# A 90 degree rotation of an 8192 x 8192 matrix: half of the outputs of most macro tiles turned by VectorE and ScalarE, and small transfers two outputs later

## The chip, the cores and the metric

The kernel runs on one core of a Trainium2 chip. The core has five engines that take instructions in order from queues of their own: PE (TensorE), DVE (VectorE), ACT (ScalarE), POOL (GpSimd) and SP (SyncE, which here only issues DMAs and waits). Semaphores order them. Sixteen DMA engines move data between the device memory and the on-chip memory SBUF (128 partitions). The metric is the device time of one execution in microseconds (us), lower is better.

## The reference

The input is a float32 matrix of 8192 x 8192 (256 MiB) and k, which is always 1:

```python
def reference(x, k):
    return np.rot90(x, k)
```

So `out[8191 - c, r] = x[r, c]`: the matrix is transposed and its row order is reversed. Nothing is computed; each element is read once and written once, 268 MB each way.

## The kernel before

The matrix is cut into 16 macro tiles of 1024 rows by 4096 columns (`kk` counts them). A macro tile is loaded by T = 8 loads of 128 rows (2 MB, 16 KB in each partition; `m` counts all 128 loads) and leaves as J = 8 outputs (`n` counts them), each one block of 512 output rows by 1024 output columns, 2 MB. Output j of a macro tile needs the chunk j (512 columns) of each of its eight loads.

The path of the data:

- SP issues the loads (L178). Two landing buffers take turns (LAND); three others hold outputs (OUTS). SP issues the next load into a buffer once VectorE has copied the previous one out of it (semaphore `s_rev`).
- VectorE copies each load, with the columns of each chunk in reverse order, into a ring of 63 slots of 512 columns (L248). A macro tile has 64 chunks, one more than there are slots. A slot is free when TensorE has transposed what it held: load m = n + 8 fills the slots that output n held. The first seven chunks wait for all of output n (`s_half`), the last one waits until the next output has begun (`s_first`), since the ring is one slot short.
- TensorE transposes 128 x 128 blocks out of the ring into PSUM (L279): 32 for each output, 16 in each of two halves (`ps0`, `ps1`). It waits for the eviction of the same half of the output before (`s_ev`).
- ScalarE evicts each half, 128 x 2048, from PSUM into an output buffer (L317), waits ahead of it until the buffer's last store has landed, and issues the store (L326).

SP's queue carries the loads and ScalarE's queue the stores, so that both directions share the sixteen DMA engines.

The last macro tile is cut otherwise, so that the end is short: its outputs take four loads (512 output columns) and two chunks each, and five buffers take turns. One of its outputs is split in two. The first part (`n_few`, the third of the last nine, n = 122) has only 64 partitions and is written by sixteen small transfers of 32 KB that SP issues (L220) behind the last load; the rest, 1.5 MB, is an output of its own (n = 123). The output that comes five later takes the same buffer and waits for all sixteen (`s_few`).

The lines in question:

```python
            begin = wide if kk == KK - 1 else 1
            cuts = [0, begin, J - 1, J] if t == T - 1 else [0, J - 1, J]
...
                got.append((lo, hi, first if hi == J else full if lo == 0 else None))
```

Of the kernel before, what the change touches and what calls it, by code (L numbers as in the profile page):

```python
# [6 lines left out]
P = 128  # L7
# [3 lines left out]
T = R // P  # L11
W = 4096
G = 4
J = W // (G * P)
# [3 lines left out]
CH = G * P  # L18
F = G * R
SLOTS = T * J - 1  # L20

END = T // 2

H = 2
# [28 lines left out]
def slot(kk, t, j):  # L53

    at = t * J + j if kk % 2 == 0 else J + t + j * T
    return (at + kk // 2 * (J + 1)) % SLOTS


def kernel(tc: tile.TileContext, x: bass.AP, k: bass.AP, out: bass.AP):
# [19 lines left out]
    n_few = n_out - J + 2  # L79
    kk, ts, js = outs[n_few]  # L80
    assert len(js) == 2 and END * P * H * G == F
    blocks = [(j, g * P, P) for j in reversed(js) for g in range(G)]
    few = [[(js[-1], g * P // 2 + h * FEW, P // 2) for g in range(G)] for h in range(H)]
    outs[n_few] = (kk, ts, js, few)
    outs.insert(n_few + 1, (kk, ts, js, [blocks[2 : 2 + G], blocks[2 + G :]]))
    n_out += 1

    def halves(n):
        if len(outs[n]) == 4:
            return outs[n][3]  # L90
        blocks = [(j, g * P, P) for j in reversed(outs[n][2]) for g in range(G)]
        return [blocks[: len(blocks) // H], blocks[len(blocks) // H :]]


    order = [(kk, a, b) for kk in range(KK) for a in range(T) for b in range(J)]
    for i, (kk, t, j) in enumerate(order):
        if i >= SLOTS:
            pk, pj, pt = order[i - SLOTS]
            assert slot(kk, t, j) == slot(pk, pt, pj)

    with tc.tile_critical():  # L101
# [9 lines left out]
        ]  # L111

# [4 lines left out]
        s_first = nc.alloc_semaphore("s_first")  # L117
        s_half = nc.alloc_semaphore("s_half")
        s_ev = nc.alloc_semaphore("s_ev")
        s_few = nc.alloc_semaphore("s_few")  # L120

# [13 lines left out]

        pieces, rev = {}, {}
        done = 0
        for m in range(n_load):  # L140
            kk, t = divmod(m, T)
            got = []
            if m >= T:
                full = (s_half, H * (m - T + 1))
                first = (s_first, m - T + 2)
            else:
                full = None
                first = (s_first, 1) if t == T - 1 else None
            begin = wide if kk == KK - 1 else 1
            cuts = [0, begin, J - 1, J] if t == T - 1 else [0, J - 1, J]  # L150
            if m < T - 1:
                cuts = [0, J]
            for lo, hi in zip(cuts[:-1], cuts[1:]):
                got.append((lo, hi, first if hi == J else full if lo == 0 else None))
                done += 1
                for j in range(lo, hi):
                    rev[m, j] = done
            pieces[m] = got

        def runs(kk, t, lo, hi):  # L160

            at = [slot(kk, t, j) for j in range(lo, hi)]
            i = 0
            while i < len(at):
                n = 1
                step = at[i + 1] - at[i] if i + 1 < len(at) else 1
                if step > 0:
                    while i + n < len(at) and at[i + n] - at[i + n - 1] == step:
                        n += 1
                else:  # L170
                    step = 1
                yield lo + i, n, at[i], step
                i += n
# [14 lines left out]
        with nc.Block() as block:  # L188
# [15 lines left out]
            @block.sync  # L204
            def _(e):
                for m in range(LAND + OUTS, n_load):
                    last = [i for i in range(m) if load_buf(i) == load_buf(m)]
                    e.wait_ge(s_rev, rev[last[-1], J - 1])
                    load(e, m)
                kk, ts, js, _ = outs[n_few]  # L210
                b = out_buf(n_few)
                top = M - macros[kk][1] - (js[-1] + 1) * CH
                left = macros[kk][0] + ts[0] * P
                rows = len(ts) * P
                for h in range(H):
                    e.wait_ge(s_ev, H * n_few + h + 1)
                    for at in (0, 2 * FEW):
                        for d in range(LEFT):
                            first = top + h * FEW + at + d
                            e.dma_start(  # L220
                                out=bass.AP(
                                    tensor=out.tensor,
                                    offset=out[first : first + 1, left : left + 1].offset,
                                    ap=[[LEFT * M, FEW // LEFT], [4 * FEW * M, G], [1, rows]],
                                ),
                                in_=bufs[b][
                                    at + d : at + FEW : LEFT, h * F // H : (h + 1) * F // H
                                ].rearrange("m (g f) -> m g f", f=rows),
                            ).then_inc(s_few, 16)
                e.wait_ge(s_few, 16 * 2 * H * LEFT)  # L230
                for b in range(LAND + OUTS):
                    n = sum(out_buf(i) == b and i != n_few for i in range(n_out))
                    if n:
                        e.wait_ge(s_store[b], 16 * n)

            @block.vector
            def _(e):
                for m in range(n_load):
                    kk, t = divmod(m, T)
                    b = load_buf(m)  # L240
                    a = bufs[b][:].rearrange("p (j c) -> p j c", c=CH)
                    e.wait_ge(s_land[b], 16 * (uses_before(m, load_buf) + 1))
                    for lo, hi, wait in pieces[m]:
                        if wait:
                            e.wait_ge(*wait)
                        for j, n, at, step in runs(kk, t, lo, hi):
                            v = ring[:, at * CH : (at + (n - 1) * step + 1) * CH]
                            i = e.tensor_copy(  # L248
                                out=bass.AP(
                                    tensor=v.tensor,  # L250
                                    offset=v.offset,
                                    ap=[v.ap[0], [step * CH, n], [1, CH]],
                                ),
                                in_=a[:, j : j + n, ::-1],
                            )
                        i.then_inc(s_rev, 1)

            @block.tensor
            def _(e):
# [8 lines left out]
                for n, (kk, ts, js, *_) in enumerate(outs):  # L268
                    parts = halves(n)
                    rows = len(ts) * P  # L270

                    def transpose(t, h, b):
                        j, off, width = parts[h][b]
                        if n:
                            wait(s_ev, H * (n - 1) + h + 1)
                        wait(s_rev, rev[kk * T + t, j])
                        at = slot(kk, t, j) * CH + off
                        f = b * rows + (t - ts[0]) * P
                        i = e.transpose(  # L279
                            ps[h][:width, f : f + P], ring[:, at : at + width], ident  # L280
                        )
                        if t == ts[-1] and b == len(parts[h]) - 1:
                            i.then_inc(s_half, 1)
                        elif t == ts[0] and h == H - 1 and b == len(parts[h]) - 1:
                            i.then_inc(s_first, 1)

                    order = [
                        (t, h, b) for h in range(H) for b in range(len(parts[h])) for t in ts
                    ]
                    if js[0] == 0:  # L290
                        order.sort()
                    for t, h, b in order:
                        transpose(t, h, b)

            @block.scalar
            def _(e):
                e.wait_ge(s_id, 2)
                e.copy(scratch, ident[:, :1])  # L298
                for n, (kk, ts, js, *_) in enumerate(outs):
                    r0, c0 = macros[kk]  # L300
                    parts = halves(n)
                    rows = len(ts) * P
                    b = out_buf(n)
                    for h in range(H):
                        if h == 0:
                            stores = [i for i in range(n) if out_buf(i) == b]
                            loads = [i for i in range(n_load) if load_buf(i) == b]
                            if stores and stores[-1] == n_few:
                                e.wait_ge(s_few, 16 * 2 * H * LEFT)
                            elif stores:  # L310
                                e.wait_ge(s_store[b], 16 * sum(i != n_few for i in stores))
                            elif loads:
                                e.wait_ge(s_rev, rev[loads[-1], J - 1])
                        e.wait_ge(s_half, H * n + h + 1)  # L314
                        width = parts[h][0][2]
                        f = len(parts[h]) * rows
                        e.copy(  # L317
                            bufs[b][:width, h * F // H : h * F // H + f], ps[h][:width, :f]
                        ).then_inc(s_ev, 1)
                    if n == n_few:  # L320
                        continue
                    groups = sum(len(part) for part in parts)
                    top = M - c0 - js[0] * CH - groups * P
                    left = r0 + ts[0] * P
                    e.wait_ge(s_ev, H * (n + 1))
# [41 lines left out]
```

## Time and profile before

The median of three runs is 1264.59 us (1264.31 to 1264.68). The profile is of one execution of its own.

| | us | of the span |
|---|---|---|
| the profiled execution's own time | 1264.36 | |
| its span, first to last instruction | 1262.3 | |
| PE busy (4,120 transposes, mean 357 ns) | 726.8 | 58% |
| ACT busy (258 evictions, mean 1867 ns) | 469.7 | 37% |
| DVE busy (313 copies, mean 1337 ns) | 403.0 | 32% |
| bytes read and written | 537 MB | 425 GB/s over the span |

The page gives the share of DMA time and the rate in 40 slices of the span; a row of a group gives the line, engine, operation, shapes and count, then busy us and mean ns, and after the second bar the idle time ahead of it with what ended it. Busy time is not the bound by itself: an engine that waits for data costs nothing as long as what it waits for never stops. The granted TensorE clock was 0.766 on the mean.

### The profile page before, as it was taken

The page shows a single profiled execution, that of the slowest core. Times are in us where ns is not written, and L with a number is a line of the kernel's source. Part 1 is how long each engine was busy: PE and PEld are TensorE (multiplying, and loading weights), DVE is VectorE, ACT ScalarE, POOL GpSimd, SP SyncE. Part 2 cuts the span into 40 slices and gives each one's busy share as a digit, 9 for nine tenths or more (in the row PEclk, how much of TensorE's full clock was granted, in tenths as well). Part 3 has the DMA queues.
Part 4 walks back from the last instruction along what each step waited for, and adds up shares of the span by engine and source line. Part 5 has one row for each costly group of instructions (what it writes and reads, how often), then busy time and mean ns, then how long its engine had stood idle before and what let it go on. Part 6 is the DMA issues. An engine that isn't in the chain of part 4 may idle for free.

```text
span 1262.3 us, 9427 instructions
## 1 busy us (share of the span) xinstructions
PE 726.8 (58%) x4120; PEld 683.2 (54%) x4120; DVE 403.0 (32%) x313; ACT 469.7 (37%) x260; POOL 0.7 (0%) x6
## 2 busy tenths in 40 slices
PE   1566566665546645566555655566555655556564
PEld 1456465665545545565554655555555654556564
DVE  3323432324323343322342233422234222442210
ACT  0343333433334333433334333343333433434364
POOL 0000000000000000000000000000000000000000
PEclk9967767676787777777777776777777777777888
DMA  9999999999999999999999999999999999999998
GB/s 399 416 430 430 428 428 429 428 430 429 428 429 428 429 429 430 427 429 432 427 428 430 430 428 428 431 429 427 430 429 428 429 429 428 430 430 428 429 412 361
DMA packets 37032, 537.48 MB, mean 426 GB/s; under 512 B 4160, under 2 KB 4160, under 8 KB 4160
## 3 DMA queue, kind: packets, MB, share of 16 engines
q10 hardware_dynamic: 18432, 267.92, 50.0%
q1 hardware_dynamic: 18560, 268.97, 49.9%
q8 instruction: 32, 0.52, 0.2%
q14 instruction: 8, 0.07, 0.0%
HBM read 268.44 MB, written 268.44 MB: 425 GB/s over the span
## 4 chain that ended last, share of the span: by engine, by line
DMA 80%; issue 8%; DVE 5%; ACT 4%; PE 1%; SPq 1%; ACTq 0%
DMA buf<-in_x_dram 70%; DMA out_dram<-buf 11%; DVE ring L248 5%; ACT buf L317 4%; PE ps L279 1%; SPq L220 1%; ACTq L326 0%; SPq L178 0%; ACTq L314 0%; SPq L362 0%; SPq L101 0%
## 5 line engine op out<-in xcount | busy, mean ns | idle before, releaser
L279 PE MATMUL ps<-head,ring 128*128 128x128 f32 x4120 | 726.8, 357 | 522.7 <-ACT buf L317 462.3
L279 PEld LDWEIGHTS ps<-head,ring 128*128 128x128 f32 x4120 | 683.2, 190 | 566.1 <-ACT buf L317 497.2
L317 ACT COPY buf<-ps 128x2048 f32<-128x2048 f32 (+1 forms) x258 | 468.3, 1867 | 781.1 <-DMA out_dram<-buf 609.3
L248 DVE COPY ring<-buf 128x512 f32<-128x512 f32 (+7 forms) x313 | 403.0, 1337 | 811.4 <-DMA buf<-in_x_dram 810.1
L298 ACT ACT_TABLE_LOAD x1 | 1.3, 1283 | 0.9 <-SPq L101 0.9
L194 POOL TENSOR_SCALAR_AFFINE_SELECT head<-head 128x128 f32<-128x128 f32 x1 | 0.3, 292 | 0.2 <-POOL head L192 0.2
L192 POOL MEMSET head<- 128x128 f32 x1 | 0.2, 205 | 0.5 <-SPq L101 0.5
L298 ACT COPY head<-head 128x1 f32<-128x1 f32 x1 | 0.2, 191 | 0.0
L348 POOL MEMSET const-bfloat16-1.0<- 128x1 bf16 x1 | 0.1, 101 | 0.0
L348 POOL MEMSET const-uint8-127<- 128x1 uint8 x1 | 0.1, 101 | 0.0
L348 POOL MEMSET const-float32-0.0<- 128x1 f32 x1 | 0.1, 100 | 0.2 <-issue 0.2
L348 POOL MEMSET const-float32-1.0<- 128x1 f32 x1 | 0.1, 98 | 0.0
## 6 DMA issues: line engine op xcount, KB each, us to landing
buf<-in_x_dram SPq DMA_DIRECT2D x128, 2048.0 KB, 16.8
out_dram<-buf ACTq DMA_DIRECT2D x127, 2048.0 KB, 25.6
out_dram<-buf ACTq DMA_DIRECT2D x1, 1536.0 KB, 9.8
out_dram<-buf SPq DMA_DIRECT2D x16, 32.0 KB
```

Of the source, the lines that this page charges most:

```text
L192: e.memset(ident, 0.0).then_inc(s_id, 1)
L194: e.affine_select(out=ident, in_=ident, compare_op=mybir.AluOpType.not_equal, fill=1.0, base=0, pattern=[[-1, P]], channel_multiplier=1,). ...
L220: e.dma_start(out=bass.AP(tensor=out.tensor, offset=out[first : first + 1, left : left + 1].offset, ap=[[LEFT * M, FEW // LEFT], [4 * FEW ...
L248: i = e.tensor_copy(out=bass.AP(tensor=v.tensor, offset=v.offset, ap=[v.ap[0], [step * CH, n], [1, CH]],), in_=a[:, j : j + n, ::-1],)
L279: i = e.transpose(ps[h][:width, f : f + P], ring[:, at : at + width], ident)
L298: e.copy(scratch, ident[:, :1])
L317: e.copy(bufs[b][:width, h * F // H : h * F // H + f], ps[h][:width, :f]).then_inc(s_ev, 1)
L348: nc = _bacc.Bacc("TRN2", target_bir_lowering=False, num_devices=1)
```

## The change

**Who turns the blocks.** In macro tiles 1 to 13 the outputs j = 1, 3, 5, 7, and in macro tile 14 j = 1, 3, 5, no longer go through TensorE and PSUM. VectorE writes their chunks into the ring by its transpose of 32 x 32 blocks in place of the copy (a second instruction for each load). When an output's buffer is free, its 16 pairs of source and destination quadrant (32 partitions each) are moved from the ring into the buffer: eight copies of 32 x 1024 by VectorE and eight by ScalarE (`moves`). VectorE does its eight ahead of the load that reuses the slots, and waits for ScalarE's eight (`s_act`) before it overwrites them. ScalarE issues the store when both are done. 55 outputs move so. Macro tiles 0 and 15 go by TensorE as before.

**The ring.** Slots now hold tile and chunk in a plain order (`slot`), and the conditions on `s_first` are gone. The chunk that has no slot, the last of a macro tile's last load, is copied in reverse into the first 512 columns of its own landing buffer; TensorE transposes it from there into the last 512 columns of `ps1` (`corner`), and ScalarE copies it into the eighth output's buffer ahead of the rest (`s_corner`, `s_freed`). The landing buffer is free again once the corner is in PSUM.

**PE's outputs.** Those of macro tiles 0 to 14 now have three parts in place of two halves (2048, 1536 and 512 columns; for j = 7 2048 less one tile of each group, and so on), since the corner holds a part of `ps1`. The third part uses `ps0` after the first has been evicted. In the last macro tile TensorE's order is by halves throughout.

**The small transfers.** `n_few` becomes the fifth of the last nine outputs (n = 124); its rest is n = 125. No later output takes its buffer.

The diff, cut to its core:

```diff
+Q = 32
+BY_DVE = 8
+BY_PE = [0, 2, 4, 6]
...
 def slot(kk, t, j):
-    at = t * J + j if kk % 2 == 0 else J + t + j * T
-    return (at + kk // 2 * (J + 1)) % SLOTS
+    return t * J + j if kk % 2 == 0 else j * J + t
...
-    n_few = n_out - J + 2
+    n_few = n_out - T + END
...
+    def by_pe(kk):
+        return list(range(J)) if kk in (0, KK - 1) else BY_PE + [J - 1] * (kk == KK - 2)
...
+        def moves(n, share):
+            kk, ts, (j,), _ = outs[n]
+            rows = len(ts) * P
+            first, step, tiles = spaced([slot(kk, t, j) for t in ts if (t, j) != (T - 1, J - 1)])
+            for a, q in share:
+                yield (
+                    at(
+                        bufs[out_buf(n)][q * Q : q * Q + Q, :],
+                        a * Q,
+                        [[rows, G], [P, tiles], [1, Q]],
+                    ),
+                    at(
+                        ring[a * Q : a * Q + Q, :],
+                        first * CH + q * Q,
+                        [[P, G], [step * CH, tiles], [1, Q]],
+                    ),
+                )
...
             @block.vector
...
+                    n = m - T
+                    if n >= 0 and moved[n]:
+                        room_for(e, n)
+                        e.wait_ge(s_rev, rev[n // J * T + T - 1 - (n % J == J - 1), n % J])
+                        for to, of in moves(n, pairs[:BY_DVE]):
+                            i = e.tensor_copy(out=to, in_=of)
+                        i.then_inc(s_dve, 1)
                     e.wait_ge(s_land[b], 16 * (uses_before(m, load_buf) + 1))
...
+                    if n >= 0:
+                        if moved[n]:
+                            e.wait_ge(s_dve, moved_until(n))
+                            e.wait_ge(s_act, moved_until(n))
+                        else:
+                            e.wait_ge(s_half, turned_until(n))
+                    for js in pieces[m]:
+                        if (m, js[0]) == (n_load - 1, J - 1):
+                            e.wait_ge(s_half, turned_until(KK * J - J))
+                        if kk < KK - 1 and (t, js[0]) == (T - 1, J - 1):
+                            e.wait_ge(s_rev, rev[m, 0])
+                            e.tensor_copy(
+                                out=at(bufs[b][:], 0, [[CH, 1], [1, CH]]), in_=landed(b, js)
+                            ).then_inc(s_rev, 1)
+                            continue
+                        turn = e.transpose if in_quadrants(kk, js[0]) else e.tensor_copy
+                        turn(out=chunk(kk, t, js), in_=landed(b, js)).then_inc(s_rev, 1)
...
             @block.scalar
...
+                    room_for(e, n)
+                    if kk < KK - 1 and js[0] == J - 1:
+                        e.wait_ge(s_corner, kk + 1)
                         e.copy(
+                            at(bufs[b][:], rows - P, [[rows, G], [1, P]]),
+                            at(corner, 0, [[P, G], [1, P]]),
+                        ).then_inc(s_freed, 1)
+                    if moved[n]:
+                        e.wait_ge(s_rev, rev[kk * T + T - 1 - (js[0] == J - 1), js[0]])
+                        for to, of in moves(n, pairs[BY_DVE:]):
+                            i = e.copy(to, of)
+                        i.then_inc(s_act, 1)
+                        e.wait_ge(s_act, moved_until(n))
+                        e.wait_ge(s_dve, moved_until(n))
```

## The prediction

> **What bounds the kernel now.** I read the page first (slices, DMA queues, groups), then the groups by form, the order of time of a middle stretch, and the windows of the last 50 us. The page says that the DMA engines are never free.
>
> ```profile
> DMA  9999999999999999999999999999999999999998
> GB/s 399 416 430 430 428 428 429 428 430 429 428 429 428 429 429 430 427 429 432 427 428 430 430 428 428 431 429 427 430 429 428 429 429 428 430 430 428 429 412 361
> q10 hardware_dynamic: 18432, 267.92, 50.0%
> q1 hardware_dynamic: 18560, 268.97, 49.9%
> q8 instruction: 32, 0.52, 0.2%
> ```
>
> 537 MB go through 16 engines at 427 to 432 GB/s from slice 3 to slice 38. At a flat 429 they would need 1252.8 us of the span's 1262.3: under 10 us belong to start and end, and no engine that computes sets the middle. The last line matters too: 32 transfers of 0.52 MB, 64 bytes for each of PE's 8,240 instructions, go over the same engines.
>
> Next, how much room each engine has in a period (one 2 MB load and one 2 MB store, 9.8 us).
>
> ```profile
> 602.36 3.64 ACT L317 COPY buf<-ps 128x2048 f32<-128x2048 f32 x2 [6.12 <-DMA out_dram<-buf]
> 603.02 4.22 DVE L248 COPY ring<-buf 128x3584 f32<-128x3584 f32 x2 [5.53 <-DMA buf<-in_x_dram]
> 612.11 3.63 ACT L317 COPY buf<-ps 128x2048 f32<-128x2048 f32 x2 [6.12 <-DMA out_dram<-buf]
> 612.79 4.22 DVE L248 COPY ring<-buf 128x3584 f32<-128x3584 f32 x2 [5.55 <-DMA buf<-in_x_dram]
> ```
>
> ScalarE and VectorE both wait for DMA more than half the period. The stretch also gives the phase: the eviction at 602.36 is the third output of its group of eight, and the load that lands at 603.02 fills the slots of the second. So the load that reuses an output's slots lands 612.79 - 602.36 = 10.4 us after that output's buffer came free.
>
> Prices, and the end:
>
> ```profile
> L248 DVE COPY ring<-buf 128x2048 f32<-128x2048 f32 x17 | 20.7, 1219 | 48.4 <-DMA buf<-in_x_dram 48.4
> L248 DVE COPY ring<-buf 128x1024 f32<-128x1024 f32 x17 | 11.7, 687 | 55.7 <-DMA buf<-in_x_dram 55.7
> L317 ACT COPY buf<-ps 128x1024 f32<-128x1024 f32 x1 | 1.0, 1018 | 0.0
> ...
> 1244.00:1249.00 5.00, 3.23 (x29) 3.19 (x30) 0.00 (x0) 4.33 (x3) 0.00 (x0) 1.00 0.93 390
> 1249.00:1254.00 5.00, 0.51 (x5) 0.27 (x3) 0.00 (x0) 2.79 (x2) 0.00 (x0) 1.00 1.00 419
> ...
> 1258.00:1259.00 1.00, 0.00 (x0) 0.00 (x0) 0.00 (x0) 0.00 (x0) 0.00 (x0) 0.50 0.71 295
> 1259.00:1260.00 1.00, 0.00 (x0) 0.00 (x0) 0.00 (x0) 0.00 (x0) 0.00 (x0) 0.50 0.16 66
> ```
>
> The last two columns of a window are DMA share and GB/s. With a full store queue the end runs at 419; in other windows it has holes, and in the last two us only some engines still work.
>
> **The change, part by part.** *VectorE in the middle.* 55 outputs move (four in each of macros 1 to 13, three in macro 14). Each adds eight 32x1024 copies. The row of that length is 0.687 us; the slow end is a copy like the 128x3584 above, 4.22 - 0.43 (the 128x512 that follows it) = 3.79 us or 1.06 ns an element, so 1.15. I take 0.687, the row of equal length: 5.5 us an output (9.2 at the slow end). The Trainium skill (VectorE: DVE Perf Modes, What auto-detection actually checks) says that a one-source fp32 copy in SBUF gets the double rate where the outermost counts are both even or equal; the trace agrees (seven chunks into a merged run: 3.79 us; the same size with seven against seven: 2.19). By it every new copy, four against four, is fast; by the slow price the sum for two loads below would be 16.0 in place of 12.3.
>
> A load's chunks become one 128x2048 copy (1.22) and one 128x2048 transpose. No row shows a transpose. Ends: 1.22 (as a fast copy) and 4.3 (twice the slow copy row, as nothing here excludes two passes); I take the slow copy row, 2048 x 1.06 = 2.2, since a block transpose is no plain copy. Two loads and one moved output, 19.6 us of DMA, cost VectorE 5.5 + 2 x 3.4 = 12.3 us. The corner copy is one more 0.43 per macro, hidden.
>
> *ScalarE.* A moved output replaces two evictions (3.64) by eight copies. The 1018 ns row reads PSUM, the new ones SBUF; bounds 0.69 (VectorE's row) and 1.87 (a whole eviction); I take 1.02, so 8.2 us. A PE output now takes three evictions: rows 1.87 and 1.02 give 0.83 ns an element plus 0.17, so 1.87 + 1.44 + 0.59 = 3.9. With 0.6 for each store issue a pair of outputs takes 13.3 of 19.6 us (20.1 at the upper bound).
>
> *Waits.* VectorE now waits ahead of a load for the store buffer, and for ScalarE's copies before it overwrites slots; the load's chunks queue behind that, and behind them SyncE's next load. The moves start when the buffer comes free and end 8.2 us later, before the load lands at 10.4: cover 2.2 us. If that is gone, the load queue runs dry only after another 9.8 - 3.4 = 6.4 us, since the next load is then still under way, and even then the store queue feeds the engines. The PE outputs' slots are free once the first eviction (1.9) and four late transposes (under 1) are done, far ahead of 10.4. The old condition on the first tiles of the next output goes. A moved store is issued some 8.8 us after its buffer came free, 4.2 before, with two stores (19.6 us) still queued: hidden. In the middle all this costs 0.
>
> *TensorE.* 4,120 transposes become 256 + 13 x 132 + 160 + 280 = 2,412. Their busy time was hidden, so 0 directly. But 3,416 fewer instructions are 0.22 MB, 13 of the 32 fetches. These took 0.2% of 16 x 1262 us, 40 us (30 to 50 by rounding): 1.25 each, 17 us for 13. Some 770 more instructions on VectorE and ScalarE, at the same 64 bytes, give 2 us back. 15/16 = 0.9 us less for each engine, if it is spread evenly; the engines that end last may lose none (0) or twice that (1.9).
>
> *The end.* The sixteen small transfers (17.4 us of issue on SyncE, a 64-partition eviction pair of 3.63 and 32 half-width transposes), and the 1.5 MB output after them, go behind two full outputs. On ScalarE's queue two whole evictions pass them: at 4.32 us an output (1209.99 to 1214.31) the store now issued at 1230.24 goes at 1226.6, 3.6 earlier; the small ones start 8 us later and land, as now, up to 6 us after the last is issued: 1243.8 + 8 = 1252, before the last store. The wait for them ahead of an eviction (chain: 7.16 us up to 1243.85, of which ScalarE idled 2.7) goes, since the ring of five buffers no longer comes back to theirs. So the last store is issued about 1247 instead of 1251.8. This fills the holes: 1224 to 1227, 1236 to 1239 and 1247 to 1249 had shares 0.85, 0.86 and 0.80, or 1.3 us in all. But it shortens the run only for engines that had the holes. By the trace's landing marks twelve engines finished the last store at 1258.7 and four at 1259.8 to 1260.2. The four show no break from 1240 on: their marks of the last four stores are 5.0 us apart. One was the slowest at every store, the other three are most likely among the four that carry the small transfers (each small transfer makes four packets, which fit between their store packets). Moving the transfers doesn't lighten these. I count 0, bounds -1.3 and +1.3 (the same holes opened for the four).
>
> *Sum:* 1264.36 (profiled; 0.23 under the median) - 0.9 + 0 = 1263.5. Own range 1261.2 to 1265.7.
>
> **The rivals.** *Faster by more than 0.2%* (under 1262.06): the fetches hit the slowest engines more than others, and the end evens out too: -1.9 - 1.3 = 1261.2. For it: the landing marks of one store drift from 1.7 us apart at the start to 11.5 near the end, so something hits some engines alone. Against: the engines with the small transfers keep their load. Another way to it would be that PE's reads had slowed the packets; windows with PE busy 5.00 and 0.60 of 5 us show 426 and 436 GB/s beside the 429 mean, which is how packets fall into windows, so I give that little. The Trainium skill (SBUF — State Buffer, SBUF: two separate sides) says that engine and DMA accesses have separate ports and cannot conflict; by it that gain is nil, as in the trace.
>
> *Slower:* VectorE becomes the bound. It decides where a pair of loads and a moved output pass 19.6 us, for example 9.2 + 2 x (1.22 + 4.3) = 20.2: 0.6 us on each of 55 pairs, +33 us, 1297. One wrong price is not enough (5.5 + 11.0 = 16.5; 9.2 + 6.8 = 16.0). For it: neither operation stands in the trace. Against: both prices must be wrong at once. A milder form is ScalarE at its 1.87 bound: 20.1 us a pair, +27 us, 1291.
>
> *Slower at the end:* the small transfers land after the last store, which decides from 1258 on. ScalarE's chain would have to slip by 6 more us; each us beyond costs one, some 1268. Against: from 1210 on ScalarE never waits longer than 3.0 us at a time.
>
> *Nothing reaches the end:* the fetches saved lie on other engines: 1264.4, inside my case.
>
> **Chances.** Forecast and no effect (within 0.2%, 1262.06 to 1267.12, about what a measurement of this kernel tells from no change): 0.50. Faster rival 0.28. VectorE or ScalarE over their budget 0.12, small transfers late 0.07, a wait that I have not seen 0.03: slower 0.22. The range goes down to 1260.5 (the faster case with 0.7 us more of the end evened out) and up to 1270 (the late transfers); the overloaded engine (0.12) and some tails stay outside.
>
> **What would show it.** Right: GB/s 427 to 432 from slice 3 to 38; q8 near 19 packets; PE x2412; VectorE and ScalarE each busy 55 to 60%, VectorE still waiting for loads; the moves under 0.7 us, transposes near 2.2, ScalarE's copies near 1.0; no eviction waiting for the small transfers; last store issued near 1247. Wrong: VectorE busy without a gap, slices under 420 in the middle, SyncE's loads issued later than 8 us after a landing, a SyncE wait that ends after the last store.

## The result, and the profile after

The changed kernel takes 1267.89 us (median of ten runs, 1267.50 to 1268.07), the kernel before 1264.54 beside it: a ratio of 1.0026, 95% interval 1.0018 to 1.0035. It is slower by 3.3 us; the forecast was 1263.5 and no difference that can be measured. The profiled execution took 1268.03 us with a span of 1266.2.

The page of the changed kernel, engines' busy times, slices and DMA queues:

```profile
PE 468.6 (37%) x2412; PEld 411.2 (32%) x2412; DVE 712.1 (56%) x719; ACT 728.9 (58%) x670; POOL 0.7 (0%) x6
...
DMA  9999999999999999999999999999999999999996
GB/s 396 415 430 430 429 429 429 430 430 428 429 430 430 430 427 430 430 430 428 429 429 429 429 429 430 429 430 430 429 430 428 429 430 429 428 430 430 429 419 291
...
q8 instruction: 19, 0.31, 0.1%
q14 instruction: 16, 0.13, 0.0%
```

The middle is untouched: 427 to 430 GB/s from slice 3 to slice 38, as before. The q8 line counts the instruction fetches of PE, packets that bring an engine its next instructions: they fell from 32 to 19, as forecast. The line below it, q14, is what the prediction did not show: fetches of 8 KB, 16 in place of 8. The same line of the kernel before:

```profile
q14 instruction: 8, 0.07, 0.0%
```

The loss stands in the last slice, 291 GB/s where it was 361. The windows of the end of the kernel before (the last three columns are TensorE's granted clock, DMA share and GB/s):

```profile
1256.00:1258.00 2.00, 0.00 (x0) 0.00 (x0) 0.00 (x0) 0.00 (x0) 0.00 (x0) 0.50 0.98 410
1258.00:1260.00 2.00, 0.00 (x0) 0.00 (x0) 0.00 (x0) 0.00 (x0) 0.00 (x0) 0.50 0.43 180
1260.00:1262.00 2.00, 0.00 (x0) 0.00 (x0) 0.00 (x0) 0.00 (x0) 0.00 (x0) 0.50 0.00 0
```

The windows of the end of the changed kernel:

```profile
1254.00:1256.00 2.00, 0.00 (x0) 0.00 (x0) 0.00 (x0) 0.00 (x0) 0.00 (x0) 0.50 0.69 287
1256.00:1258.00 2.00, 0.00 (x0) 0.00 (x0) 0.00 (x0) 0.00 (x0) 0.00 (x0) 0.50 0.33 139
1258.00:1260.00 2.00, 0.00 (x0) 0.00 (x0) 0.00 (x0) 0.00 (x0) 0.00 (x0) 0.50 0.16 66
1260.00:1262.00 2.00, 0.00 (x0) 0.00 (x0) 0.00 (x0) 0.00 (x0) 0.00 (x0) 0.50 0.12 49
1262.00:1264.00 2.00, 0.00 (x0) 0.00 (x0) 0.00 (x0) 0.00 (x0) 0.00 (x0) 0.50 0.08 33
```

Before, all engines stop within some two us. After, most stop between 1255 and 1259, and from 1260 to 1262 the share is 0.12 = 2/16: two DMA engines work alone for some five us, and one of them for one more. Each of the sixteen leaves a landing mark for each store, and those of the last store say the same (us, sorted; the marks carry no engine's name):

```
before 1259.1 x8, 1259.2 x4, 1260.2, 1260.2, 1260.5, 1260.6
after  1255.5 1255.5 1255.6 1255.7 1255.7 1256.0 1256.1 1256.1 1257.1 1257.2 1257.4 1257.7 1258.6 1258.6 1263.4 1264.6
```

Fourteen engines are done earlier than before, two are 3 to 4 us later, and the last one sets the time. In every run below the median lies 3.3 to 4.0 us above the last mark of its profile.

### The profile page after: what moved, and what is told of

Read it like the earlier page. It is cut to its first block, busy times and chain, and to the rows that moved or that the text cites. A ratio compares the mean times of both kernels' runs of the same rounds, so it can differ in the third digit from the quotient of the medians.

```text
span 1266.2 us, 6966 instructions
## 1 busy us (share of the span) xinstructions
PE 468.6 (37%) x2412; PEld 411.2 (32%) x2412; DVE 712.1 (56%) x719; ACT 728.9 (58%) x670; POOL 0.7 (0%) x6
## 4 chain that ended last, share of the span: by engine, by line
DMA 78%; DVE 11%; issue 5%; ACT 3%; PE 1%; ACTq 0%; SPq 0%
DMA buf<-in_x_dram 75%; DVE ring L334 11%; DMA out_dram<-buf 4%; ACT buf L416 3%; PE ps L377 1%; DVE buf L315 0%; ACTq L428 0%; ACT buf L397 0%; SPq L247 0%; ACTq L410 0%; SPq L464 0%; SPq L126 0%; ACTq L407 0%
## 5 line engine op out<-in xcount | busy, mean ns | idle before, releaser
L377 PE MATMUL ps<-head,ring 128*128 128x128 f32 (+1 forms) x2352 | 455.8, 371 | 776.4 <-ACT buf L416 591.9
L377 PEld LDWEIGHTS ps<-head,ring 128*128 128x128 f32 (+1 forms) x2352 | 398.4, 196 | 833.5 <-ACT buf L416 637.4
L404 ACT COPY buf<-ring 32x1024 f32<-32x1024 f32 (+1 forms) x440 | 447.1, 1016 | 196.4 <-DMA out_dram<-buf 191.6
L334 DVE COPY ring<-buf 128x2048 f32<-128x2048 f32 (+4 forms) x152 | 182.4, 1201 | 496.6 <-DMA buf<-in_x_dram 493.5
L416 ACT COPY buf<-ps 128x2048 f32<-128x2048 f32 (+4 forms) x213 | 271.7, 1345 | 241.0 <-PE ps L377 117.0
L315 DVE COPY buf<-ring 32x1024 f32<-32x1024 f32 (+1 forms) x440 | 291.8, 663 | 5.3
L334 DVE STREAM_TRANSPOSE ring<-buf 128x2048 f32<-128x2048 f32 (+1 forms) x112 | 246.8, 2204 | 0.0
L397 ACT COPY buf<-ps 128x512 f32<-128x512 f32 x15 | 8.8, 585 | 79.9 <-DMA out_dram<-buf 79.9
L365 PE MATMUL ps<-head,buf 128*128 128x128 f32 x60 | 15.9, 420 | 0.0
L365 PEld LDWEIGHTS ps<-head,buf 128*128 128x128 f32 x60 | 13.0, 229 | 0.0
```

The lines of the kernel that those rows point to most:

```text
L315: i = e.tensor_copy(out=to, in_=of)
L334: turn(out=chunk(kk, t, js), in_=landed(b, js)).then_inc(s_rev, 1)
L365: i = e.transpose(corner[:, g * P : g * P + P], bufs[load_buf(m)][:, g * P : g * P + P], ident,)
L377: i = e.transpose(ps[h][:width, to : to + P], chunk(kk, t, [j])[:, 0, off : off + width], ident,)
L397: e.copy(at(bufs[b][:], rows - P, [[rows, G], [1, P]]), at(corner, 0, [[P, G], [1, P]]),).then_inc(s_freed, 1)
L404: i = e.copy(to, of)
```

## Which engines are late, and why

The time of each fetch packet can be set beside the number of instructions that an engine had run, and beside the stores in which one DMA engine fell back against the other fifteen. After, q14 has a packet at 147.8, 312.2, 473.0, 636.1, 793.2, 960.0 and 1115.9 us, where VectorE had run 61, 194, 318, 446, 570, 705 and 833 instructions, so one for each 128 or so (8 KB are 128 times 64 bytes). These counts take in the instructions that only wait. Followed from store to store by the marks, one and the same DMA engine fell back by 0.95 to 1.00 us at the last six of these times (at the first, a packet of PE falls into the same stretch, and the two engines that fell back can't be told apart). A second series, at 136.6, 280.0, 435.6 and so on to 1217.6, goes with each 128 instructions of ScalarE, eight packets, and another engine falls back by 0.5 to 0.9 at most of them. One more packet, at 611.5, belongs to neither series; the kernel before has its like at 679.1. Before, VectorE had three such packets (186.5, 519.2, 862.4) and ScalarE four. PE's packets of 16 KB set one engine back by 1.4 to 1.7 us each time, and not always the same. From 473 to 1212 us none of PE's packets set VectorE's engine back, so it gained nothing there from PE's fewer fetches; from 639 us on it is the last at every store.

The Trainium skill (Runtime: NRT & Kernel Launch, Instruction fetch mechanics) says that the sequencer fetches ahead by a DMA queue of its own and that the cost is "mostly hidden". The trace agrees for the engine that fetches (no wait for it shows), but not for a kernel that is bound by DMA: here each fetch is 0.5 to 1.7 us on one of sixteen DMA engines. It gives blocks of 256 instructions; the packets of VectorE and ScalarE here stand for 128.

The small transfers are the other half. The Trainium skill (DMA: Bandwidth & Descriptors, Why a DMA increments its semaphore by 16 and not by 1) says that a transfer runs on the largest number of engines up to 16 that divides its slowest dimension, here 4, and on the lowest-numbered ones; so sixteen transfers load the same four engines. The trace agrees on the count: the sixteen leave 80 landing marks, five each (the four engines and one for the rest). No run here shows the numbers of the four; that the two late engines are among them shows when the small transfers are taken out (e3 below). By the packets' times (four of 8 KB in each, 0.315 us) each of the four carries 16 x 0.315 = 5.0 us more, and all sixteen save 1.2 by the smaller store.

Theory T1: the end is set by the DMA engine on which the fetches and the small transfers add up. Theory T2 adds the series above: VectorE's and ScalarE's fetches fall on two fixed engines, and both are among the four. VectorE's engine got 4 x 0.95 = 3.8 us more than before. If its mark before was one of the four late ones (1260.2 to 1260.6), that gives 1264.0 to 1264.4; measured 1264.6. Rivals: R1, the later place of the small transfers (with the ring's order and the corner) costs the 3.3 us; R2, the moves, transposes and waits on VectorE and ScalarE do; R3, the fetches count, but spread over all engines.

## Experiments

**Small transfers moved, or taken out.** e1 is the kernel before with them in the fifth of the last nine outputs, e2 the changed kernel with them in the third (and the wait of the output that reuses the buffer, as before). e3 and e4 are the two kernels without them: the output goes whole.

```diff
# e1
-    n_few = n_out - J + 2
+    n_few = n_out - T + END
# e2
-    n_few = n_out - T + END
+    n_few = n_out - J + 2
...
+            if stores and stores[-1] == n_few:
+                e.wait_ge(s_few, 16 * 2 * H * LEFT)
# e3 (e4 likewise, of the kernel before); SyncE's loop that issues them goes too
-    n_few = n_out - T + END
...
-    outs[n_few] = (kk, ts, js, few)
-    outs.insert(n_few + 1, (kk, ts, js, blocks[H:]))
-    n_out += 1
+    n_few = None
```

> The kernel before with one edit: the small transfers move from the third to the fifth of the last nine outputs. Theory T1 (the end is set by the DMA engine on which the small transfers and the instruction fetches add up; here neither the four engines of the small transfers nor the fetches change): 1264.5 us, at most 0.8 us either way. Rival R1 (the later position itself costs the 3.3 us): 1267.9. Rival R2 (the new path through VectorE and ScalarE costs it): 1264.5, as T1.

> The changed kernel with the small transfers back in the third of the last nine outputs. T1: the fetches are those of the changed kernel and the four engines are the same, so the two slow engines stay slow: 1267 to 1268 us. R1 (position): 1264.5. R2 (the new path): 1268.

> The changed kernel without small transfers: the fifth of the last outputs is written whole, 2 MB, by ScalarE's queue. T1: each of the four engines gets 131 KB less and 33 KB more, 3.9 us by the packets' times, so the engine that ended last (landing mark 1264.6) ends near 1260.7 and the time is near 1264.0. R1: 1264.5, since there is no position. R2: 1268, since the middle is unchanged.

> The kernel before without small transfers, its outputs whole. T1: the twelve engines that ended early get 33 KB more, 1.2 us, and the one of them that is the slowest sets the end: 1265.2 to 1265.8 us. A plain balance that counts every engine as equal: 1259.1 + 1.2, which is under the 1260.6 of before, so 1264.0 or less. R1 and R2 say nothing of this one.

Measured: e1 1265.95 (ratio to before 1.0009, 1.0000 to 1.0017), e2 1267.69 (1.0025, 1.0015 to 1.0035), e3 1264.22 (0.9998, 0.9989 to 1.0007; T1 had 1264.0), e4 1265.42 (1.0007, 0.9998 to 1.0016; T1 had 1265.2 to 1265.8). The end of e3:

```profile
1258.00:1260.00 2.00, 0.00 (x0) 0.00 (x0) 0.00 (x0) 0.00 (x0) 0.00 (x0) 0.50 0.08 33
1260.00:1262.00 2.00, 0.00 (x0) 0.00 (x0) 0.00 (x0) 0.00 (x0) 0.00 (x0) 0.50 0.00 0
```

e3 decides against R2: the whole new path is still there, and the cost is gone. The two latest marks are 1259.4 and 1260.5, 4.0 and 4.1 under what they were with the small transfers (1263.4 and 1264.6; 5.0 - 1.2 = 3.8 by the packets' times). e4 (last mark 1261.9) and e3 together say what the whole change is worth where no small transfers stand in the way: it gains 1.2 us (the spans of all executions are 1263.0 to 1263.7 and 1261.8 to 1262.4). That the saved fetches of PE make this gain is argued, not shown. e2 is as T1 has it (1267 to 1268), but not a clean one: its wait for the transfers holds the last store back too. e1 fits no theory well: 1.4 us over T1's figure, 1.9 under R1's. ScalarE's order of time in e1 shows why:

```profile
1229.56 3.62 ACT L317 COPY buf<-ps 64x2048 f32<-64x2048 f32 x2 [2.96 <-PE ps L279]
...
1237.17 2.78 ACT L317 COPY buf<-ps 128x2048 f32<-128x2048 f32 x2 [4.00 <-PE ps L279]
...
1253.43 0.55 ACTq L326 DMA_DIRECT2D out_dram<-buf  x1
```

ScalarE waits 2.96 and 4.00 us for TensorE, which in that kernel turns both halves of an output of first chunks in step; the last store goes at 1253.4, later than before (1251.82), and all engines end with it (1261.4 to 1262.4). That left open whether the place costs something; e13 and e14 below take it up.

**Fetches alone.** The kernel before with four copies of one column (128x1) added on ScalarE for each output, on VectorE for each load, or both. They write unused columns beside the identity. VectorE also waits once, at its start, for the identity (`s_id`); nothing else is touched.

```diff
+TINY = 4
# at VectorE's start (e5, e7)
+                e.wait_ge(s_id, 2)
# after a load's chunks, on VectorE (e5, e7)
+                    for i in range(TINY):
+                        c = P + 16 + m % 16 * TINY + i
+                        e.tensor_copy(out=head[:, c : c + 1], in_=ident[:, :1])
# after a store's issue, on ScalarE (e5, e6)
+                    for i in range(TINY):
+                        c = P + 1 + n % 2 * TINY + i
+                        e.copy(head[:, c : c + 1], ident[:, :1])
```

> The kernel before with four copies of one column (128x1, to unused columns beside the identity) added on ScalarE and on VectorE for each of the outputs and loads: 516 and 512 more instructions, no other edit; the matrix goes as before. Theory T2 (VectorE's and ScalarE's instruction fetches of 8 KB fall always on the same two DMA engines, which are among the four that carry the small transfers): about 8 more packets in q14 (8 to 16), 4 on each of the two engines at 0.65 to 0.98 us each, so the engine that ends last ends 2.6 to 3.9 us later, if it is one of the two: 1267 to 1268.5 us. Rival R2 (it is the moves, transposes and waits of the new path that cost the 3.3 us): 1264.5, as tiny copies fill idle time. Rival R3 (fetches are spread over all engines): 8 x 0.9 / 16 = 0.5 us, 1265.0.

> As the one before, on ScalarE alone (516 more instructions). T2: 4 more packets in q14, all on one engine: 1266.5 to 1268.5 if ScalarE's engine is the one that ends last, otherwise 1264.5. R2: 1264.5. R3: 1264.8.

> As the one before, on VectorE alone (512 more instructions). T2: 4 more packets in q14, all on one engine: 1266.5 to 1268.5 if VectorE's engine is the one that ends last, otherwise 1264.5; of this run and the one with ScalarE at least one shows the cost. R2: 1264.5. R3: 1264.8.

Measured: e5 1268.41 (1.0031, 1.0019 to 1.0043), e6 1266.50 (1.0015, 1.0007 to 1.0024), e7 1268.12 (1.0028, 1.0017 to 1.0039). The groups of e7 and its queue of fetches:

```profile
L262 DVE COPY head<-head 128x1 f32<-128x1 f32 x512 | 42.2, 146 | 0.0
...
q14 instruction: 12, 0.10, 0.0%
```

512 copies that take 42 us of an engine that is idle for two thirds of the run make the kernel slower by as much as the change did, with no transpose or move in it, and no new wait but the one at the start; they bring four fetches (8 to 12), 128 instructions each. In the kernel before, the delay reaches the end by another way, though. ScalarE's order of time in the kernel before, from the eviction that waits for the small transfers to the last store:

```profile
1243.85 3.63 ACT L317 COPY buf<-ps 128x2048 f32<-128x2048 f32 x2 [2.71 <-DMA out_dram<-buf]
...
1251.82 0.55 ACTq L326 DMA_DIRECT2D out_dram<-buf  x1
```

The same in e7:

```profile
1246.40 3.64 ACT L323 COPY buf<-ps 128x2048 f32<-128x2048 f32 x2 [5.19 <-DMA out_dram<-buf]
...
1252.08 1.87 ACT L323 COPY buf<-ps 128x2048 f32<-128x2048 f32 x1 [2.05 <-PE ps L285]
...
1256.40 0.55 ACTq L332 DMA_DIRECT2D out_dram<-buf  x1
```

The small transfers land 2.5 us later on the slow engine, the eviction waits for them, and TensorE, idle meanwhile, is granted half its clock, as a window of e7 shows:

```profile
1250.00:1252.00 2.00, 2.00 (x12) 2.00 (x10) 0.00 (x0) 0.03 (x1) 0.00 (x0) 0.50 0.61 262
```

Twelve transposes in 2.0 us, where before at full clock 32 took 3.74. The last store is issued 4.6 us later and all engines end with it (1262.9 to 1264.4). So these three show that more instructions on idle engines are enough, but a size for one fetch can't be read from them. The changed kernel has no such wait, so the same copies were added to it.

> The changed kernel with four copies of one column (128x1) added on VectorE for each load, 512 more instructions, no other edit. T2: the engine that ended last at 1264.6 is the one that carries VectorE's fetches (seven events of 0.95 us on one engine); 4 more packets in q14 end it 3.8 us later, and nothing else moves: landing mark near 1268.4, 1271.7 us. R2 (moves and waits of the path): 1268. R3 (fetches spread over all engines): 1268.1.

> The changed kernel with four copies of one column added on ScalarE for each output, 516 more instructions. T2: the engine that ended second last at 1263.4 is the one that carries ScalarE's fetches, 0.65 to 0.9 us each; 4 more packets in q14 end it 2.6 to 3.6 us later, 1266.0 to 1267.0, past VectorE's 1264.6: 1269.3 to 1270.4 us. R2 and R3: 1268.

Measured: e9 1271.46 (1.0054, 1.0040 to 1.0068), e10 1268.84 (1.0033, 1.0020 to 1.0045). The end of e9:

```profile
1262.00:1264.00 2.00, 0.00 (x0) 0.00 (x0) 0.00 (x0) 0.00 (x0) 0.00 (x0) 0.50 0.10 41
1264.00:1266.00 2.00, 0.00 (x0) 0.00 (x0) 0.00 (x0) 0.00 (x0) 0.00 (x0) 0.50 0.06 25
1266.00:1268.00 2.00, 0.00 (x0) 0.00 (x0) 0.00 (x0) 0.00 (x0) 0.00 (x0) 0.50 0.04 16
```

A share of 0.06 is one engine. Its mark is 1268.1 (1268.4 expected), and the second latest stays at 1263.6: VectorE's fetches all fall on that one engine, and R3 (1268.1 here, 1265.0 in e5) falls with it. In e10 the two latest marks are 1264.2 and 1265.5. Followed from store to store, the later one falls back by 0.67, 0.67 and 0.80 us at ScalarE's fetches at 724.6, 1038.9 and 1138.3 us, the other by 0.96 or 0.97 at VectorE's at 793.4, 960.2 and 1116.1, so the later one is ScalarE's. At the end it has moved from 1263.4 by 2.0 us for four fetches, 0.5 each and less than the 0.65 that was the low end; the time is 0.5 under the range for the same reason.

**Small transfers on more engines.** LEFT = 1 makes four transfers of sixteen packets, LEFT = 2 eight of eight, out of the same bytes.

```diff
-LEFT = 4
+LEFT = 1    # e8; LEFT = 2 in e11
```

> The changed kernel with LEFT = 1: the 0.5 MB of the small transfers go as four transfers of 16 packets each, where before each of sixteen transfers had 4 packets. They stay where they are, in the fifth of the last nine outputs, on SP. T2 (a transfer of 4 packets always loads the same four engines, and two of these are the two with the fetches): all 16 engines carry the same again, as in the run without small transfers: 1264.0 to 1264.6. R2: 1267.9, since the path is unchanged. If spread over 16 engines did not matter: 1267.9.

> The changed kernel with LEFT = 2: eight small transfers of 8 packets each in place of sixteen of 4. T2: eight engines carry 32 KB more each than they lose, 1.3 us, in place of four with 98 KB more, 3.9 us; if the two with the fetches are among the eight, the end is at 1264.6 - 2.6 = 1262.0: 1265.3 us, up to 1.4 more if the transfers with more packets slow the others as those of sixteen did (332 GB/s at 1235 to 1240). If they are not among the eight: 1264.0. R2: 1267.9.

Measured: e8 1266.25 (1.0014, 1.0005 to 1.0023), e11 1266.76 (1.0018, 1.0009 to 1.0026). Both are faster than the changed kernel, which R2 excludes, but e8 is 1.7 us above what T2 said. Two windows of e8, while its small transfers run:

```profile
1230.00:1235.00 5.00, 3.85 (x35) 3.62 (x35) 0.00 (x0) 3.58 (x3) 0.00 (x0) 1.00 1.02 392
1235.00:1240.00 5.00, 4.58 (x40) 4.07 (x38) 0.00 (x0) 4.33 (x3) 0.00 (x0) 1.00 0.99 332
```

The engines are busy, but move 392 and 332 GB/s in place of 419 (e3 at 1235 to 1240). From 1235 to 1240 the small packets took 0.62 us on the mean (0.315 in the changed kernel) and the 16 KB ones beside them 0.71 (0.63). Not all are slow: the 16 KB ones' median is 0.63 in both. (27 + 87) x 5 us / 419 = 1.4 us is lost that way on each engine, which takes the expected last mark from 1260.5 to 1261.9; measured 1262.5, so 0.6 stays unexplained. e11 is at the upper end of what was expected (1265.3, up to 1.4 more): in the windows 1230 to 1235, 1235 to 1240 and 1240 to 1245 it moves 403, 384 and 416 GB/s, (16 + 35 + 3) x 5 us / 419 = 0.6 us lost, and its last mark is 1263.5 where 1262.0 + 0.6 would be 1262.6. Why some packets are slow was not tried and stays open.

**Half the moves, no small transfers.** The moves stay in macro tiles 1, 3, ... 13 alone.

```diff
# e12, on top of e3
-        return list(range(J)) if kk in (0, KK - 1) else BY_PE + [J - 1] * (kk == KK - 2)
+        return list(range(J)) if kk % 2 == 0 or kk == KK - 1 else BY_PE
```

> The changed kernel without small transfers, and with the moves in macro tiles 1, 3, ... 13 alone (28 outputs in place of 55), all else by TensorE. T2, from the marks of the two kernels without small transfers: the engine with VectorE's fetches gets two fewer (1260.5 - 1.9 = 1258.6), the engines with PE's fetches lie between 1259 and 1261, so about 1260: 1263.5 us, a little under both kernels. R2 (cost goes with the number of moved outputs, half of 3.3): 1265.7 without regard to the small transfers.

Measured: 1263.88 (0.9995, 0.9986 to 1.0003), last marks 1259.9 and 1260.1 (about 1260 expected), 25 fetches of PE and 13 in q14. It has the lowest median of all that ran, but the interval does not tell it from the kernel before. R2's 1265.7 falls.

**The place, once more.** e13 is the changed kernel with every output by TensorE; all else of the change stays. e14 is e1 with TensorE's order by halves in the last macro tile.

```diff
# e13
-        return list(range(J)) if kk in (0, KK - 1) else BY_PE + [J - 1] * (kk == KK - 2)
+        return list(range(J))
# e14, on top of e1
-                    if js[0] == 0:
+                    if js[0] == 0 and kk < KK - 1:
                         order.sort()
```

> The changed kernel with every output by TensorE: no transposes on VectorE, no moves; the ring's order, the corner, the three parts of an output, the order by halves and the small transfers in the fifth of the last nine outputs stay. T2: VectorE has three to four fetches fewer, so its engine ends near 1264.6 - 3.5 x 0.95 = 1261.3; ScalarE has about two fewer (three evictions and a corner an output), 1263.4 - 1.3 = 1262.1; PE has 32 again: 1264.5 to 1265.5 us. R1 (the fifth position, with what else stays): 1267.9.

> The kernel before with the small transfers in the fifth of the last nine outputs, as in the first run, and TensorE's order by halves in the last macro tile, as the changed kernel has it. In the first run ScalarE idled 2.96 and 4.00 us for TensorE ahead of the small output and the next, since TensorE turned both halves of these together. T2: that wait goes, the last store is issued some 4 us earlier, and the engines end by their own load near 1260.8: 1264.0 to 1264.6 us. R1 (the position itself): 1266 as in the first run, or 1267.9.

Measured: e13 1264.78 (1.0001, 0.9992 to 1.0010), last mark 1260.8, 9 packets in q14; e14 1264.48 (0.9999, 0.9990 to 1.0008), last mark 1260.9 (1260.8 expected). ScalarE in e14:

```profile
1231.54 2.78 ACT L317 COPY buf<-ps 128x2048 f32<-128x2048 f32 x2 [0.35 <-PE ps L279]
...
1247.80 0.55 ACTq L326 DMA_DIRECT2D out_dram<-buf  x1
```

The wait of 4.00 us is 0.35, and the last store goes 5.6 us earlier than in e1. R1 falls: place, ring, corner and order cost nothing that can be measured. e14 also shows what the move of the small transfers was worth by itself: nothing. The last store goes 4 us earlier than before, and the end does not move, since it is set by the load of single engines.

## Why the prediction was wrong, point by point

*The middle stays bound by DMA and costs 0.* Right. 429 GB/s, and VectorE and ScalarE still wait for loads and stores.

*The prices.* Right, all of them. (The two copies read as 3.79 and 2.19 us out of merged rows took 3.89 and 2.29 singly; the price of a transpose stays 2.2 by it.) The changed kernel's groups by form:

```profile
L404 ACT COPY buf<-ring 32x1024 f32<-32x1024 f32 x336 | 349.9, 1041 | 195.0 <-DMA out_dram<-buf 191.6
L315 DVE COPY buf<-ring 32x1024 f32<-32x1024 f32 x336 | 228.1, 679 | 4.1
L334 DVE STREAM_TRANSPOSE ring<-buf 128x2048 f32<-128x2048 f32 x91 | 209.7, 2304 | 0.0
L416 ACT COPY buf<-ps 128x2048 f32<-128x2048 f32 x78 | 145.0, 1867 | 238.1 <-PE ps L377 114.0 <-DVE buf L315 88.4 <-DMA out_dram<-buf 30.6
L416 ACT COPY buf<-ps 128x1536 f32<-128x1536 f32 x63 | 91.1, 1445 | 0.2 <-PE ps L377 0.2
L416 ACT COPY buf<-ps 128x512 f32<-128x512 f32 x63 | 38.1, 604 | 0.0
```

ScalarE's move 1.04 us (1.02 taken), VectorE's 0.68 (0.687), the transpose 2.30 (2.2), evictions 1.87, 1.45 and 0.60 (1.87, 1.44, 0.59); both engines busy 56 and 58% (55 to 60).

*The waits in a period.* Right in the sum, but not in the order. A stretch of the changed kernel's order of time:

```profile
611.60 8.41 ACT L404 COPY buf<-ring 32x1024 f32<-32x1024 f32 x8 [5.02 <-DMA out_dram<-buf]
612.88 1.23 DVE L334 COPY ring<-buf 128x2048 f32<-128x2048 f32 x1 [6.28 <-DMA buf<-in_x_dram]
614.02 2.30 DVE L334 STREAM_TRANSPOSE ring<-buf 128x2048 f32<-128x2048 f32 x1
616.25 5.52 DVE L315 COPY buf<-ring 32x1024 f32<-32x1024 f32 x8
...
622.50 3.70 ACT L416 COPY buf<-ps 128x2048 f32<-128x2048 f32 x3 [2.49 <-DVE buf L315]
```

The buffer comes free while VectorE waits for a load, so it takes that load's chunks first and does its moves after, which end 10.2 us after the buffer came free; ScalarE then waits 2.5 us for them (88.4 us in all, the group above), and VectorE waits only 0.88 us for the next load, at 622.65. The prediction had the moves done ahead of the load, 2.2 us before it landed. The cover, stores queued and 5 to 6 us of slack on either engine, held.

*ScalarE at the end.* Right: last store issued at 1247.23 (some 1247 forecast), no wait for the small transfers, and these landed by 1254.7 (1252 forecast), before the last store did. The rival "small transfers late" did not come. ScalarE's last store in the changed kernel:

```profile
1247.23 1.42 ACTq L428 DMA_DIRECT2D out_dram<-buf  x1
```

*The fetches: "15/16 = 0.9 us less for each engine, if it is spread evenly; the engines that end last may lose none (0) or twice that (1.9)".* This is the step that failed. The count was near: 13 fetches of PE less as forecast, and 8 smaller ones more where 770 instructions of 64 bytes make 6. (By the prediction's own price these 770 give 3.8 us back and not 2, which makes the term 0.8; that is not what failed.) But the new fetches are not spread at all: four each go to two fixed engines, and PE's, of which there are fewer, did not fall on the one that ends last (none from 473 to 1212 us). The bounds 0 and 1.9 left out that an engine could get more than before; it got 3.8. The term was -0.9 and measured +4.0 on the last mark, +3.3 in the time.

*The end, counted 0.* The reading behind it was half right: of the four late engines three "are most likely among the four that carry the small transfers", and moving the transfers "doesn't lighten these". What it did not ask is what else these four carry. The 2 us by which 770 more instructions lessen the gain were spread over sixteen engines in the paragraph on TensorE, though the marks of one store, 11.5 us apart and used for the faster rival, already said that something hits some engines alone. That q14 had its own line in the profile of before (8 packets) was not used. The marks of the last store that the prediction gives (1258.7, and 1259.8 to 1260.2) are 0.4 us lower than on the span's scale (1259.1, and 1260.2 to 1260.6); nothing hangs on that.

*The rivals and the range.* None of the rivals is what happened. The result lies outside the sum's own range, 1261.2 to 1265.7. The wide range, up to 1270, held it by luck: its upper end was there for a mechanism that did not come.

## What to carry to other kernels

In this kernel, where all sixteen DMA engines are busy from end to end, the time was set by the engine with the most work, not by the sum over sixteen. In one like it, look at the landing marks of the last store, engine by engine, and price whatever falls on a few engines (instruction fetches, transfers with few packets) on those engines. An instruction on an idle engine was not free: here 128 on VectorE cost one DMA engine 0.95 us, and 512 one-column copies cost the kernel 3.6 us. A small transfer that evens out the end in one version may load the very engine that the next version has made late, so it is to be weighed again after each change of the instruction counts.

## What the runs showed of the hardware that was not expected

- VectorE's fetches (8 KB, one for 128 instructions) fall on one DMA engine each time, ScalarE's on another, PE's (16 KB) on changing ones; each sets its engine back by some 0.95, 0.5 to 0.9, and 1.4 to 1.7 us in a stream of 16 KB packets of 0.61 us.
- While small transfers with sixteen packets of 8 KB each ran, the engines were busy but moved 332 GB/s in place of 419, and the mean packet was slower (16 KB: 0.71 us in place of 0.63; e8). With four packets each the packets were not slower (0.63 us, and 0.315 for the small ones), and 410 and 398 GB/s in the same two windows of the changed kernel go with DMA shares of 0.98 and 0.96.
- A wait of 5.2 us ahead of the eviction that frees PSUM left TensorE idle, took its granted clock to 0.50, and the next output's transposes kept ScalarE waiting 2.05 us, 0.67 before (e7).
